# Layer-norm operands loaded in four parts behind weight chunks, and the state-space shuffles issued from ScalarE, in a two-layer hybrid trunk

## The chip, the core and the metric

The kernel runs on one core of a Trainium2 chip. The metric is the device time of one execution in microseconds (us); lower is better. Five engines matter: TensorE (PE) multiplies, VectorE (DVE), ScalarE (ACT) and GpSimd (POOL) do elementwise work, and SyncE (SP) mostly issues DMA transfers. Each engine runs its instructions in the order in which they stand in its own queue, so an issue that must wait holds up all issues behind it.

## The reference

256 tokens of width 1024 pass through two layers. A layer mixes tokens in three ways (RWKV-7, latent attention, a diagonal state space model called S5), merges the three under gates, projects by `w_out`, adds the residual and normalizes; then a SwiGLU feed-forward network, residual and normalization again. All is in float32.

```python
for l in range(DEPTH):
    p = x @ w_in[l]
    ...
    merged = gates[..., 0, :] * y_a + gates[..., 1, :] * y_b + gates[..., 2, :] * y_c
    x = layer_norm(DEEPNORM_ALPHA * x + merged @ w_out[l], ln1_g[l], ln1_b[l])
    h = jax.nn.silu(x @ ffn_w1[l]) * (x @ ffn_w3[l])
    x = layer_norm(DEEPNORM_ALPHA * x + h @ ffn_w2[l], ln2_g[l], ln2_b[l])
```

## The kernel before

**Weights.** All large weights lie in one DRAM array of chunks, 138 per layer, most of them 128x1024 float32 (512 KB). `w_load` brings a chunk in: SP issues a DMA into `raw` (L160), ACT casts it to the high part `whi` (L161), DVE (for some columns POOL, L173) subtracts to get the low part `wlo` (L171). There are 3 buffers of `raw` and 4 of each part, and `w_next` keeps 4 chunks loaded ahead of use. Each product is three matmuls: high by high, high by low, low by high (L203 to L205; in `token_major` L487 to L489). So PE can run only as long as chunks arrive and are split, and a chunk's DMA can start only when the cast and the subtraction have freed one of the 3 `raw` buffers.

**The two projections that end in a normalization** are done by `token_major`: `w_out` with 8 chunks and the second FFN matrix ("ffn2") with 22. Tokens lie on partitions, and four accumulators of 128x512 are kept: two token blocks b0 and b1 by two column halves n0 and n1 (`mm`, `mm`, `mm`, and one named `pc`). The last four chunks are held, and the code runs them for b0n0, then b0n1, b1n0 and b1n1, so that `layer_norm` of b0 can begin while PE still works on b1. `layer_norm` adds the residual `xk` (L446), takes statistics (L448, L449), gets the inverse root (L235 on DVE, L237 on POOL), centres and scales by `lg` (L453), and scales and shifts by `lb` (L460). Then PE transposes the result (L467), ACT copies it out as `xh`, and DVE makes its low part `xl` (L470). The next product's first matmuls (L1270 to L1272 in ffn1) need both. The new residual is written to DRAM as `xd`, from which the next `token_major` loads it.

**The order** of instructions on each engine is set by a scheduler that may move an instruction ahead of others on its engine wherever data and buffers allow. That holds for the loads of `lg`, `lb` (512 KB each, one row repeated on all partitions) and `xk` (1 MB), which stand in `token_major` at step `k == at`: `at` is 2 for `w_out` and 12 for ffn2. Their memory comes from a pool that takes over space used by others before: for ffn2 of layer 0 that of temporaries (`st`, `ct`, `t`, L430 to L434) which POOL uses to make the sine tables of layer 1's S5.

**The S5 input.** The product `u` is copied out of PSUM by ACT (L113) and shuffled over partitions into `U2` by 8 DMAs of 64 KB each (L671, issued from SP), from which PE's first S5 products (L702) read.

Of the kernel before, what the change touches and what calls it, by code (L numbers as in the profile page):

```python
# [17 lines left out]
D = 1024  # L18
# [68 lines left out]
def trunk(ctx: ExitStack, tc: tile.TileContext, xT, xtok, ws, spA, spB, spC, sp5, lnv, cst, out, dbg=None,  # L87
          layers=L, mark=None):
    nc = tc.nc
    V, S, PE, SY, G = nc.vector, nc.scalar, nc.tensor, nc.sync, nc.gpsimd  # L90
# [14 lines left out]
    def mmps():  # L105
        return pmm.tile([128, 512], F32, tag="mm", name="mm")

    def mxps(k):
        return pmx.tile([128, 512], F32, tag="p" + k, name="p" + k, bufs=1 if k == "c" else 2)

    def cp(k, out, in_):

        {"S": S.copy, "V": V.tensor_copy, "G": G.tensor_copy}[CPE[k]](out=out, in_=in_)  # L113
# [36 lines left out]
    state = {"next": 0}  # L150
# [5 lines left out]
    def w_load(i, hi, lo):  # L156
        w = LAT if i in lat_chunks else CH
        raw = wp.tile([128, CH], F32, tag="raw", name="raw", bufs=WRAW)
        for s in (slice(0, w // 2), slice(w // 2, w)) if i == 0 else (slice(0, w),):
            SY.dma_start(out=raw[:, s], in_=ws[i, :, s])  # L160
            S.copy(out=hi[:, s], in_=raw[:, s])  # L161
            if i == 0:
                V.tensor_tensor(out=lo[:, s], in0=raw[:, s], in1=hi[:, s].bitcast(F32), op=ALU.subtract)
        if i == 0:
            return
        if gate:

            V.tensor_copy(out=lo[:, 0:1], in_=gate.pop())
        n, j = divmod(i, CHUNKS_PER_LAYER)
        m = w * int(GS[24 * n + j // 3]) // 8 if j < 72 else w  # L170
        V.tensor_tensor(out=lo[:, 0:m], in0=raw[:, 0:m], in1=hi[:, 0:m].bitcast(F32), op=ALU.subtract)  # L171
        if m < w:
            G.tensor_tensor(out=lo[:, m:w], in0=raw[:, m:w], in1=hi[:, m:w].bitcast(F32), op=ALU.subtract)  # L173

    def w_early(pool, i):

        w = LAT if i in lat_chunks else CH
        early[i] = t = pool.tile([128, w], F32R, name=f"eh{i}"), pool.tile([128, w], F32R, name=f"el{i}")
        w_load(i, *t)

    def w_prefetch():
        i = state["next"]
        if i >= nchunks:
            return
        state["next"] = i + 1
        if i not in early:
            hi = wp.tile([128, CH], F32R, tag="whi", name="whi", bufs=WHI)
            lo = wp.tile([128, CH], F32R, tag="wlo", name="wlo", bufs=WHI)
            w_load(i, hi, lo)
            wq.append((hi, lo))  # L190
        else:
            wq.append(early[i])

    def w_next(ahead=AHEAD):
        while sum(w not in early.values() for w in wq) < ahead:
            if state["next"] >= nchunks:
                break
            w_prefetch()
        return wq.pop(0)
# [20 lines left out]
    def proj_pair(x, nk=8):  # L220
        ps = mmps()
        for j in range(2):
            proj(w_next(), 0, x, nk, ps[:, 256 * j:256 * j + 256])
        return ps
# [19 lines left out]
    with tc.tile_pool(name="xin", bufs=1) as q:  # L244
        xr = q.tile([128, 8, T], F32, name="xr")
        for i in range(4):
            s = slice(2 * i, 2 * i + 2)
# [8 lines left out]
        for i in range(4):  # L256
            s = slice(2 * i, 2 * i + 2)
            S.copy(out=xh[:, s], in_=xr[:, s])
            V.tensor_tensor(out=xl[:, s], in0=xr[:, s], in1=xh[:, s].bitcast(F32), op=ALU.subtract)  # L259
    x_dram = xtok  # L260
# [213 lines left out]
    def token_major(a, nk, ln, last, q, l, at):  # L474

        nonlocal x_dram
        lg = q.tile([128, D], F32, tag="lg", name="lg")
        lb = q.tile([128, D], F32, tag="lb", name="lb")
        xk = q.tile([128, 2, D], F32, tag="xk", name="xk")
        acc = [[mmps(), mmps()], [mmps(), mxps("c")]]  # L480

        def run(w, k, b, ns=(0, 1)):
            t = slice(128 * b, 128 * b + 128)
            for n in ns:
                s = slice(512 * n, 512 * n + 512)
                ah, al = a[0][:, k, t], a[1][:, k, t]
                PE.matmul(acc[b][n], lhsT=ah, rhs=w[0][:, s], start=(k == 0), stop=False)  # L487
                PE.matmul(acc[b][n], lhsT=ah, rhs=w[1][:, s], start=False, stop=False)  # L488
                PE.matmul(acc[b][n], lhsT=al, rhs=w[0][:, s], start=False, stop=(k == nk - 1))  # L489

        for k in range(nk - NST):
            if k == at:
                SY.dma_start(out=lg, in_=lnv[l, ln:ln + 1, :].to_broadcast([128, D]))
                SY.dma_start(out=lb, in_=lnv[l, ln + 1:ln + 2, :].to_broadcast([128, D]))
                SY.dma_start(out=xk, in_=x_dram)
            w = w_next()
            for b in range(2):
                run(w, k, b)
        wst = [w_next(NST - i) for i in range(NST)]
        ln_ = []  # L500
        for b in range(2):
            for n in range(2):
                for i in range(NST):
                    run(wst[i], nk - NST + i, b, (n,))
            ln_.append(layer_norm(q, xk, b, acc[b], lg, lb, last, 4 * LN_EPS))
            next(ln_[b])
            if (LNL if last else LNO) == 0:
                next(ln_[b])
        if (LNL if last else LNO) == 1:
            next(ln_[0])  # L510
            next(ln_[1])
        if not last:
            xd = dr.tile([128, 2, D], F32, tag=f"xd{l}{ln}", name=f"xd{l}{ln}")
            SY.dma_start(out=xd, in_=xk)
            x_dram = xd
# [4 lines left out]
    for l in range(layers):  # L520
# [136 lines left out]
        with tc.tile_pool(name=f"s5p{l}", bufs=1, side=P) as q:  # L657
            u = q.tile([128, 4, 2, 128], F32, tag="u", name="u")
            U2 = q.tile([128, 8, 128], F32, tag="U2", name="U2")

            def s5_in(fp):
                mark("s5proj")
                ps = proj_pair(X)
                for i in range(2):
                    cp(5, out=u[:, 2 * fp:2 * fp + 2, i, :], in_=ps.rearrange("p (f c i) -> p f i c", f=2, i=2)[:, :, i, :])
                if fp == 0:
                    return
                for j in range(4):
                    for i in range(2):
                        r = 64 * (j % 2) + 32 * i  # L670
                        SY.dma_start(out=U2[r:r + 32, j // 2::2, :], in_=u[32 * j:32 * j + 32, :, i, :])  # L671

            tgen = []

# [78 lines left out]
            def s5_gelu(i):  # L753
# [7 lines left out]
                else:  # L761
# [5 lines left out]
                V.tensor_tensor(out=yS[1][:, s], in0=g, in1=yS[0][:, s].bitcast(F32), op=ALU.subtract)  # L767

            run = {"S": s5_in, "T": s5_tables0, "m": lat, "N": lambda _: mla_norm(q, lts[0]), "r": rw_unit, "P": layer_params, "t": s5_tile,
                   "g": s5_gelu, "G": lambda fp: gate_pair(2, fp, M[:, 2 * fp:2 * fp + 2])}  # L770
            gens = {}
# [30 lines left out]
        q = mixed.enter_context(tc.tile_pool(name=f"rw{l}", bufs=1, side=P))  # L802
        if True:
# [288 lines left out]
            for i in range(2):  # L1092
                r = slice(64 - 32 * i, 96 - 32 * i)
# [111 lines left out]
            gate0 = {}  # L1205
# [36 lines left out]
        dump("M", M)  # L1242
        with tc.tile_pool(name=f"mg{l}", bufs=1, side=P) as q:
            mark("wout")
            token_major(gate0[1], 8, 0, False, q, l, 2)
        gstack.close()


# [2 lines left out]
        with tc.tile_pool(name=f"ff{l}", bufs=1, side=O) as q:  # L1251
# [13 lines left out]
            for b in range(2):  # L1265
                ps = mmps()
                t = slice(128 * b, 128 * b + 128)
                for k in range(8):
                    w, s = w4[k // 2], slice(512 * (k % 2), 512 * (k % 2) + 512)
# [36 lines left out]
            with tc.tile_pool(name=f"mh{l}", bufs=1, side=P) as q2:  # L1306
                token_major((hh, hl), NF, 2, l == layers - 1, q2, l, 12)
# [181 lines left out]
```

## Time and profile before

| quantity | value |
|---|---|
| time, median of 3 runs | 1088.11 us (1084.67 to 1090.08) |
| profiled execution: time | 1090.58 us |
| profiled execution: span, first to last instruction | 1088.9 us |
| mean granted TensorE clock, share of full speed | 0.972 |
| PE busy | 1026.9 us (94%) |
| DVE / ACT / POOL busy | 802.8 / 477.3 / 231.5 us |
| chain of work that ended last | PE 61%, DVE 17%, POOL 10%, DMA 5%, ACT 3%, issue 3% |
| landing after issue, median: `raw` / `lg` / `lb` / `xk` from `xd` | 4.1 / 5.1 / 5.7 / 7.9 us |

The profiled execution took 2.47 us longer than the median run. Its span begins with the first instruction and ends with the last, 1.7 us short of the time. Times in the text such as "at 449" are us from the start of the span; layer 0 reaches to about 565, layer 1 from there on. Where a queue's row says xN, the N instructions stand behind one another and the length reaches to the end of the last.

### The profile page before, as it was taken

Reading aid. Unit: us, or ns where it says so; the run is one execution under the profiler, and the core shown is the slowest. Engines: PE = TensorE matmul, PEld = TensorE weight load, DVE = VectorE, ACT = ScalarE, POOL = GpSimd, SP = SyncE. Lnnn points to the kernel's source line nnn. Section 1 sums busy time; section 2 is a strip of 40 time slices with the busy share of each in tenths; the row PEclk is TensorE's granted clock in tenths of the full one; section 3 lists DMA queues with packets and bytes.
Section 4 is the critical chain, followed back from the end, with each engine's and each line's share of the span. In section 5 each row is a group of like instructions: output and inputs, shape, how many; then the busy total and the mean of one; then the engine's idle time right before and its main releaser. Section 6 shows DMA issues by size and latency. Waiting matters only on the chain.

```text
span 1088.9 us, 21216 instructions
## 1 busy us (share of the span) xinstructions
PE 1026.9 (94%) x8560; PEld 923.8 (85%) x8560; DVE 802.8 (74%) x1560; ACT 477.3 (44%) x789; POOL 231.5 (21%) x254
## 2 busy tenths in 40 slices
PE   9489999999999999899998999999999899999997
PEld 8378887888897899798878999878889779999985
DVE  7599988977478799576473898789756866676645
ACT  5243387544343344244325345765334433434331
POOL 2941042210000599400011003221002420000000
PEclk9789999999999999999998899999999999999999
DMA  7342262132285655466545325222225746555552
GB/s 279 98 140 86 95 192 73 59 118 96 81 291 183 204 173 167 178 209 217 184 143 177 115 80 173 90 97 79 79 98 169 243 152 230 186 183 180 186 195 78
DMA packets 47683, 164.91 MB, mean 151 GB/s; under 512 B 5729, under 2 KB 8289, under 8 KB 46689
## 3 DMA queue, kind: packets, MB, share of 16 engines
q1 hardware_dynamic: 47296, 163.03, 45.2%
q8 instruction: 67, 1.10, 0.4%
q10 hardware_dynamic: 288, 0.52, 0.1%
q14 instruction: 32, 0.25, 0.1%
HBM read 157.77 MB, written 4.19 MB: 149 GB/s over the span
## 4 chain that ended last, share of the span: by engine, by line
PE 61%; DVE 17%; POOL 10%; DMA 5%; ACT 3%; issue 3%; SPq 0%; DVEq 0%; ACTq 0%; POOLq 0%
PE mm L205 11%; PE mm L204 11%; PE mm L203 11%; DMA raw<-in_ws 4%; PE mm L488 3%; PE mm L489 3%; PE mm L487 3%; DVE wlo L171 3%; ACT whi L161 2%; DVE z L721 2%; POOL st L432 1%; POOL st L434 1%; PE pa L702 1%; POOL t L430 1%; PE pa L916 1%
## 5 line engine op out<-in xcount | busy, mean ns | idle before, releaser
L171 DVE TENSOR_TENSOR wlo<-raw,whi 128x1024 fp32r<-128x1024 f32 (+2 forms) x265 | 336.7, 1277 | 175.3 <-ACT whi L161 173.2
L161 ACT CAST whi<-raw 128x1024 fp32r<-128x1024 f32 (+2 forms) x267 | 277.5, 1043 | 386.0 <-PE mm L204 207.3
L203 PE MATMUL mm<-xh,whi 128*128 128x256 f32 x1312 | 379.5, 289 | 14.2 <-ACT whi L161 14.1
L205 PE MATMUL mm<-xh,wlo 128*128 128x256 f32 x1312 | 378.3, 289 | 2.1 <-DVE wlo L171 1.9
L204 PE MATMUL mm<-xl,whi 128*128 128x256 f32 x1312 | 379.3, 289 | 0.4 <-DVE xl L259 0.4
L203 PEld LDWEIGHTS mm<-xh,whi 128*128 128x128 f32 x1312 | 252.5, 192 | 18.7 <-ACT whi L161 14.7
L205 PEld LDWEIGHTS mm<-xh,wlo 128*128 128x128 f32 x1312 | 253.5, 193 | 6.1 <-DVE wlo L171 2.9
L204 PEld LDWEIGHTS mm<-xl,whi 128*128 128x128 f32 x1312 | 252.4, 192 | 3.9 <-issue 1.8
L237 POOL TENSOR_TENSOR rs<-rs,mhalf 128x1 f32<-128x1 f32 x8 | 7.8, 970 | 344.0 <-DVE rs L235 344.0
L203 PE MATMUL mm<-yh,whi 128*128 128x256 f32 x256 | 74.5, 291 | 0.1
L205 PE MATMUL mm<-yh,wlo 128*128 128x256 f32 x256 | 74.1, 290 | 0.0
L204 PE MATMUL mm<-yl,whi 128*128 128x256 f32 x256 | 74.1, 289 | 0.0
L488 PE MATMUL mm<-wlo,hh 128*128 128x512 f32 x132 | 52.0, 394 | 0.0
L487 PE MATMUL mm<-whi,hh 128*128 128x512 f32 x132 | 51.6, 394 | 0.0
L489 PE MATMUL mm<-whi,hl 128*128 128x512 f32 x132 | 51.5, 393 | 0.0
L203 PEld LDWEIGHTS mm<-yh,whi 128*128 128x128 f32 x256 | 48.5, 189 | 2.3 <-ACT qa L113 0.9
L204 PEld LDWEIGHTS mm<-yl,whi 128*128 128x128 f32 x256 | 48.5, 189 | 1.2 <-issue 0.8
L205 PEld LDWEIGHTS mm<-yh,wlo 128*128 128x128 f32 x256 | 48.6, 190 | 1.1 <-issue 0.7
L173 POOL TENSOR_TENSOR wlo<-raw,whi 128x384 fp32r<-128x384 f32 (+2 forms) x24 | 29.5, 1236 | 72.4 <-ACT whi L161 72.4
L237 POOL TENSOR_TENSOR rsn<-rsn,mhalf 128x8 f32<-128x8 f32 x4 | 6.5, 1634 | 142.8 <-DVE rsn L235 142.8
L923 POOL TENSOR_SCALAR_AFFINE_SELECT Mk<-Mk 64x512 f32<-64x512 f32 x32 | 27.0, 844 | 43.6 <-ACT Mk L113 42.3
L487 PEld LDWEIGHTS mm<-whi,hh 128*128 128x128 f32 x132 | 24.8, 188 | 6.1 <-DVE th L1260 0.7
(498 smaller groups left out, 1764.2 us busy)
## 6 DMA issues: line engine op xcount, KB each, us to landing
raw<-in_ws SPq DMA_DIRECT2D x267, 512.0 KB, 4.1
raw<-in_ws SPq DMA_DIRECT2D x8, 416.0 KB, 3.5
xd<-xk SPq DMA_DIRECT2D x3, 1024.0 KB, 4.1
xk<-xd SPq DMA_DIRECT2D x3, 1024.0 KB, 7.9
lg<-in_lnv SPq DMA_DIRECT2D x4, 512.0 KB, 5.1
lb<-in_lnv SPq DMA_DIRECT2D x4, 512.0 KB, 5.7
pc<-in_spC SPq DMA_DIRECT2D x2, 768.0 KB, 5.1
pb<-in_spB SPq DMA_DIRECT2D x2, 512.0 KB, 5.2
```

What stands on the lines that cost most here:

```text
L161: S.copy(out=hi[:, s], in_=raw[:, s])
L171: V.tensor_tensor(out=lo[:, 0:m], in0=raw[:, 0:m], in1=hi[:, 0:m].bitcast(F32), op=ALU.subtract)
L173: G.tensor_tensor(out=lo[:, m:w], in0=raw[:, m:w], in1=hi[:, m:w].bitcast(F32), op=ALU.subtract)
L203: PE.matmul(ps, lhsT=wh, rhs=xh, start=first, stop=False)
L204: PE.matmul(ps, lhsT=wh, rhs=xl, start=False, stop=False)
L205: PE.matmul(ps, lhsT=wl, rhs=xh, start=False, stop=last)
L237: G.tensor_tensor(out=out, in0=in_, in1=mh(out), op=ALU.pow)
L487: PE.matmul(acc[b][n], lhsT=ah, rhs=w[0][:, s], start=(k == 0), stop=False)
L488: PE.matmul(acc[b][n], lhsT=ah, rhs=w[1][:, s], start=False, stop=False)
L489: PE.matmul(acc[b][n], lhsT=al, rhs=w[0][:, s], start=False, stop=(k == nk - 1))
L721: V.tensor_tensor_scan(out=z[:, pp, qq, ri], data0=bc(m2[:, j:j + 1], [128, 128]), data1=z[:, pp, qq, ri], initial=0.0, op0=ALU.mult, op1= ...
L923: G.affine_select(out=Mk[r, h], in_=Mk[r, h], pattern=[[0, 4], [1, 2], [1, 64]], compare_op=ALU.is_ge, fill=0.0, base=-1, channel_multipli ...
```

## The change

The load of `lg`, `lb` and `xk` becomes four loads of 512 KB: the half of `xk` for b0, `lg`, `lb`, the half of `xk` for b1. One is issued at each of the steps k = at to at + 3, and `tc.issue_after` holds it in the queue behind the newest weight chunk's DMA (`state["dma"]`), so the scheduler cannot move it ahead. For `w_out`, `at` goes from 2 to 0; for ffn2 it stays 12. The 8 shuffles into `U2` are issued from ACT's queue instead of SP's.

```diff
@@ w_load
-            SY.dma_start(out=raw[:, s], in_=ws[i, :, s])
+            state["dma"] = SY.dma_start(out=raw[:, s], in_=ws[i, :, s])
@@ token_major
+        loads = [(xk[:, 0], x_dram[:, 0]), (lg, lnv[l, ln:ln + 1, :].to_broadcast([128, D])),
+                 (lb, lnv[l, ln + 1:ln + 2, :].to_broadcast([128, D])), (xk[:, 1], x_dram[:, 1])]
         for k in range(nk - NST):
-            if k == at:
-                SY.dma_start(out=lg, in_=lnv[l, ln:ln + 1, :].to_broadcast([128, D]))
-                SY.dma_start(out=lb, in_=lnv[l, ln + 1:ln + 2, :].to_broadcast([128, D]))
-                SY.dma_start(out=xk, in_=x_dram)
             w = w_next()
+            if at <= k < at + 4:
+
+                with tc.issue_after(state["dma"].ins if hasattr(state["dma"], "ins") else state["dma"]):
+                    SY.dma_start(out=loads[k - at][0], in_=loads[k - at][1])
@@ s5_in
-                        SY.dma_start(out=U2[r:r + 32, j // 2::2, :], in_=u[32 * j:32 * j + 32, :, i, :])
+                        S.dma_start(out=U2[r:r + 32, j // 2::2, :], in_=u[32 * j:32 * j + 32, :, i, :])
@@ the call for w_out
-            token_major(gate0[1], 8, 0, False, q, l, 2)
+            token_major(gate0[1], 8, 0, False, q, l, 0)
```

SP's queue in layer 0 between the table inputs of the next layer (`cd`) and the end of the layer held this before (a chunk of 832 columns is one of layer 1 that is loaded early, the others are those of ffn1 and ffn2):

```order
-L376 DMA cd<-in_spB 128x1024
-L160 DMA raw<-in_ws 128x1024 x22
-L493 DMA lg<-in_lnv 128x1024
-L494 DMA lb<-in_lnv 128x1024
-L495 DMA xk<-xd_4229 128x2048
-L160 DMA raw<-in_ws 128x1024 x14
-L160 DMA raw<-in_ws 128x832 x2
-L160 DMA raw<-in_ws 128x1024 x19
```

With the change the same stretch reads:

```order
+L376 DMA cd<-in_spB 128x1024
+L160 DMA raw<-in_ws 128x1024 x36
+L160 DMA raw<-in_ws 128x832 x2
+L160 DMA raw<-in_ws 128x1024 x13
+L498 DMA xk<-xd_4230 128x1024
+L160 DMA raw<-in_ws 128x1024
+L498 DMA lg<-in_lnv 128x1024
+L160 DMA raw<-in_ws 128x1024
+L498 DMA lb<-in_lnv 128x1024
+L160 DMA raw<-in_ws 128x1024
+L498 DMA xk<-xd_4230 128x1024
 L160 DMA raw<-in_ws 128x1024 x3
```

The 2 MB that stood in one block, 22 chunks behind `cd`, now stand 51 chunks behind it, in ffn2, each part between two chunks.

In layer 1 the end of `w_out` and ffn1 read so before (`xd_6293` is the residual of `w_out`, `xd_10152` that of ffn2; `lg` for `w_out` stands right ahead of this piece):

```order
 L160 DMA raw<-in_ws 128x1024 x3
-L494 DMA lb<-in_lnv 128x1024
-L160 DMA raw<-in_ws 128x1024 x3
-L495 DMA xk<-xd_6293 128x2048
-L160 DMA raw<-in_ws 128x1024 x9
-L493 DMA lg<-in_lnv 128x1024
-L160 DMA raw<-in_ws 128x1024 x2
-L494 DMA lb<-in_lnv 128x1024
-L160 DMA raw<-in_ws 128x1024
-L514 DMA xd_10152<-xk 128x2048
-L160 DMA raw<-in_ws 128x1024 x3
```

and now the loads of `w_out` stand so, with those of ffn2 another 53 chunks behind:

```order
+L160 DMA raw<-in_ws 128x1024 x35
+L498 DMA xk<-xd_6295 128x1024
+L160 DMA raw<-in_ws 128x1024
+L498 DMA lg<-in_lnv 128x1024
+L160 DMA raw<-in_ws 128x1024
+L498 DMA lb<-in_lnv 128x1024
+L160 DMA raw<-in_ws 128x1024
+L498 DMA xk<-xd_6295 128x1024
+L160 DMA raw<-in_ws 128x1024 x4
+L516 DMA xd_10155<-xk 128x2048
```

The 1 MB of `xk` for `w_out` stood 9 chunks ahead of the first load for ffn2, and that one (issued at 872.27) went out while PE still worked on `w_out`. Now only `w_out`'s own loads lie there, 5 to 12 chunks later than before.

The scheduler also changes PE's order at the end of `w_out` of layer 0 (`mm_4040` is the accumulator b0n0, `mm_4041` b0n1, `mm_4042` b1n0, `pc_4043` b1n1; `msh` and `msl` are the two parts of the merged input). Before, the two last matmuls for `mm_4040` and those that follow were these, with 24 more for b1 behind them:

```order
L488 MATMUL mm_4040<-wlo_4120,msh_3298 128x512
L489 MATMUL mm_4040<-whi_4119,msl_3299 128x512
L487 MATMUL mm_4041<-whi_4101,msh_3298 128x512
L488 MATMUL mm_4041<-wlo_4102,msh_3298 128x512
L489 MATMUL mm_4041<-whi_4101,msl_3299 128x512
L487 MATMUL mm_4041<-whi_4119,msh_3298 128x512
L488 MATMUL mm_4041<-wlo_4120,msh_3298 128x512
L489 MATMUL mm_4041<-whi_4119,msl_3299 128x512
```

Now the ten last matmuls of `w_out` are these:

```order
L488 MATMUL mm_4040<-wlo_4121,msh_3298 128x512
L489 MATMUL mm_4040<-whi_4120,msl_3299 128x512
L488 MATMUL mm_4041<-wlo_4121,msh_3298 128x512
L489 MATMUL mm_4041<-whi_4120,msl_3299 128x512
L488 MATMUL mm_4042<-wlo_4121,msh_3298 128x512
L489 MATMUL mm_4042<-whi_4120,msl_3299 128x512
L489 MATMUL pc_4043<-whi_4101,msl_3299 128x512
L487 MATMUL pc_4043<-whi_4120,msh_3298 128x512
L488 MATMUL pc_4043<-wlo_4121,msh_3298 128x512
L489 MATMUL pc_4043<-whi_4120,msl_3299 128x512
```

The last matmul for b0n0 stood 30 matmuls ahead of the end and now stands 8 ahead of it; that of b0n1 24, now 6; b1n0 12, now 4. In layer 1 the same distances go from 36, 24 and 12 to 18, 16 and 12.

## Rows read from the trace of the kernel before

**Rows 1.** Part 1 of the page: busy us of the engines (share of the span).

```profile
PE 1026.9 (94%) x8560; PEld 923.8 (85%) x8560; DVE 802.8 (74%) x1560; ACT 477.3 (44%) x789; POOL 231.5 (21%) x254
```

**Rows 2.** Timeline of SP's queue, 430 to 465: start, length, instructions.

```profile
430.28 6.84 SPq L160 DMA_DIRECT2D raw<-in_ws  x3
449.29 0.33 SPq L493 DMA_DIRECT2D lg<-in_lnv  x1
...
450.14 0.42 SPq L495 DMA_DIRECT2D xk<-xd  x1
450.67 13.72 SPq L160 DMA_DIRECT2D raw<-in_ws  x5
```

**Rows 3.** Chain that ended last, 445 to 470: start, length, what.

```profile
447.12 2.15 POOL st L434
...
450.67 8.25 DMA raw<-in_ws
...
460.10 1.24 DVE wlo L171
```

**Rows 4.** Windows: PE, PEld, DVE, ACT, POOL busy (x); clock, DMA share, GB/s.

```profile
455.50:460.20 4.70, 0.15 (x2) 0.08 (x1) 0.10 (x1) 1.18 (x2) 0.00 (x0) 1.00 0.98 404
460.20:467.20 7.00, 6.42 (x29) 6.12 (x30) 6.80 (x12) 3.51 (x5) 0.00 (x0) 0.51 0.51 173
467.20:478.00 10.80, 10.80 (x92) 10.80 (x91) 8.34 (x13) 4.76 (x6) 0.00 (x0) 1.00 0.78 227
```

**Rows 5.** Timeline of PE, 350 to 362: start, length, line, [idle before <-releaser].

```profile
352.78 0.40 PE L489 MATMUL pc<-whi,msl 128*128 128x512 f32 x1
353.02 1.04 PE L467 MATMUL pa<-c,xk 128*128 128x128 f32 x8
354.59 0.50 PE L1270 MATMUL mm<-eh,xh 128*128 128x512 f32 x1 [0.53 <-ACT xh L113]
...
355.31 0.50 PE L1272 MATMUL mm<-eh,xl 128*128 128x512 f32 x1
```

**Rows 6.** Timeline of DVE, 344 to 360, the same columns.

```profile
346.21 0.69 DVE L446 SCALAR_TENSOR_TENSOR xk<-xk,mm 128x512 f32<-128x512 f32 x1 [0.97 <-PE mm L489]
...
349.38 1.41 DVE L453 SCALAR_TENSOR_TENSOR xk<-xk,mv,lg 128x512 f32<-128x512 f32 x2
...
354.57 0.69 DVE L470 TENSOR_TENSOR xl<-pa,xh 128x512 fp32r<-128x512 f32 x1
```

**Rows 7.** Windows, columns of rows 4, over other stretches.

```profile
859.20:890.60 31.40, 26.16 (x99) 20.33 (x99) 21.20 (x29) 10.56 (x12) 11.64 (x8) 0.89 0.57 188
865.40:878.00 12.60, 12.52 (x47) 9.85 (x47) 7.52 (x8) 4.19 (x4) 6.25 (x4) 0.86 0.77 245
591.00:607.00 16.00, 16.00 (x66) 14.43 (x67) 6.40 (x12) 2.95 (x4) 0.00 (x0) 0.50 0.26 81
300.00:320.00 20.00, 20.00 (x169) 20.00 (x169) 13.76 (x17) 9.29 (x12) 2.13 (x5) 1.00 0.86 305
```

**Rows 8.** Timeline of PE, 858 to 896.

```profile
865.37 0.50 PE L487 MATMUL mm<-whi,msh 128*128 128x512 f32 x1 [3.18 <-DVE gate L796]
```

**Rows 9.** Chain that ended last, 846 to 896.

```profile
850.28 7.37 DMA raw<-in_ws
...
871.89 6.16 DMA raw<-in_ws
...
892.85 0.50 PE mm L1272
```

**Rows 10.** Timeline of SP's queue, 580 to 612.

```profile
587.07 5.12 SPq L671 DMA_DIRECT2D U<-u  x8
```

**Rows 11.** Timeline of PE, 585 to 594.

```profile
590.91 1.19 PE L702 MATMUL pa<-U,bl 64*128 64x128 f32 x4 [3.99 <-DMA U<-u]
```

**Rows 12.** Timeline of ACT, 583 to 600.

```profile
597.29 1.04 ACT L161 CAST whi<-raw 128x1024 fp32r<-128x1024 f32 x1 [7.66 <-PE mm L204]
```

**Rows 13.** Timeline of PE, 40 to 80.

```profile
55.86 0.31 PE L413 MATMUL pb<-cd,bd 128*32 128x32 f32 x2 [7.33 <-DVE bd L383]
```

## The prediction

> **What bounds the kernel now.** The page's first part comes first: PE is busy 94% of the span [rows 1], so only places where PE stands still, or runs at a lower clock, can give time back, and any new stand costs its full length. I then looked for PE's idle gaps near the instructions that the change touches: the loads in layer 0's ffn1, the two ends of `w_out`, and the shuffles of layer 1. (Layer numbers are 0 and 1.)
>
> The largest gap is at 449. SP issued its last chunk DMA before it at about 437, and then nothing until 449.29, when `lg` went out [rows 2]. The chain of waits says why: it runs through POOL's `st L434`, which ends at 447.12 + 2.15 = 449.27 [rows 3]. That is the last of the sine-table operations whose temporaries lie in the memory that `lg` is to take. So `lg` waited for POOL, and every chunk behind it in SP's queue waited too, though the chunks themselves had free buffers. Then 2 MB of `lg`, `lb` and `xk` travelled ahead of the next chunk, which was issued at 450.67 and took 8.25 us to land; its low part ended at 461.34 [rows 3]. The windows show what PE lost: nearly no work for 4.7 us, then 7.0 us with 29 matmuls at a granted clock of 0.51, near the lower level of 1.2 GHz, then 92 in 10.8 us at full clock (2.4 GHz), or 0.117 us each [rows 4].
>
> At the end of `w_out` of layer 0 PE hardly stands still: the last matmul is issued at 352.78, the transposes follow at 353.02, and the first matmul of ffn1 that needs `xl` (L1272) starts at 355.31 [rows 5]. DVE began to normalize b0 at 346.21, seven us ahead of PE's end [rows 6]; that is what the order "b0n0 first" buys.
>
> In layer 1 `w_out` takes 31.4 us [rows 7] for 96 matmuls. At the pitch between the rows at 352.78 and 353.02, 0.24 us, they need 23.0: 8.4 us are lost there. The chain names two chunk DMAs with long flights, 7.37 us and 6.16 us [rows 9]. The first left SP right behind the 1 MB of `xk`; the second travelled with ffn2's `lg`. The first delays ACT and DVE and so the gate product on which PE waits 3.18 us [rows 8], and at 865.4 to 878 the clock is 0.86 [rows 7].
>
> **The change, part by part.** I count gains as positive.
>
> *Layer 0, loads of ffn2.* They move 29 chunks later, past the end of the tables. Chunks at 437 to 450 no longer wait for POOL. In the 11.7 us of the first two windows of [rows 4] PE did 2 + 29 = 31 matmuls, worth 31 x 0.117 = 3.6 us at full clock: 8.1 us lost, and **+8.0** taken, with +6 (half of the slow-clock part comes back elsewhere) to +9 as bounds. The work that hides the loads at their new place is PE's: a ffn2 chunk is 12 matmuls of 0.24 us, 2.8 us, and at the 404 GB/s of the loaded window [rows 4] a chunk plus a 512 KB load takes 2 x 1.3 = 2.6 us. So the parts just fit, with four chunks in reserve; if they do not, see the second rival.
>
> *Layer 0, loads of `w_out`.* Before, they cost nothing: in 300 to 320 PE is busy 20.00 of 20 us [rows 7]. Now they stand among `w_out`'s own chunks, with the same 2.6 against 2.8 us. I take 0 for the transfer. But the scheduler's new order of PE has a price. The last matmul of b0n0 stands 8 ahead of the end in place of 30, so DVE starts about 8 x 0.24 - 0.1 = 1.8 us ahead of PE's end E, not 7.0. Before, from the start of the first L446 to the start of L470 it took 354.57 - 346.21 = 8.36 us [rows 6]. Now three more instructions of b1 stand in front of that L470 on DVE: two L453 (1.41 us together [rows 6]) and one more statistics or aggregate step of about 0.2 to 0.7 us. That makes about 9.9. The low part of b0 starts at E - 1.8 + 9.9 = E + 8.1 and ends 0.69 later, at E + 8.8; L1272 follows. Before it started at 355.31, which is E + 2.13 with E = 353.18 (352.78 + 0.40). So **-6.7**, with bounds -5 and -8. PE stands still for most of it. What the clock then does is bounded by three rows: after an idle of 3.18 us the next 12.6 us ran at 0.86, a loss of 12.6 x 0.14 = 1.8 us [rows 7, 8]; after the stand at 449 7.0 us ran at 0.51, a loss of 3.4 [rows 4]; after 3.99 us idle 16 us ran at 0.50, a loss of 8 [rows 7, 11]. I take **-2.0**, near the first, since PE has transposes and a few matmuls inside its idle time; bounds 0 and -8.
>
> *Layer 1, `w_out`.* Its own loads come 5 to 12 chunks later and those of ffn2 are out of it. The two flights exceed the median of 4.1 us by 3.3 and 2.1, together 5.4 us; all of the loss is 8.4. I take **+7.0**, since the lower clock comes with the waits, and keep +3 (its own four loads now travel with the last chunks) to +8.4. The tail costs here as well: b0n0 ends 18 matmuls ahead of the end, so DVE starts about 18 x 0.24 - 0.2 = 4.1 us ahead of E. With b1's statistics less crowded than in layer 0, L446 to the end of L470 is the 9.05 us of before (355.26 - 346.21), so `xl` is there at E + 4.95. Before, L1272 started at 892.85 [rows 9] with E = 890.60 (the end of the window in [rows 7]), so at E + 2.25: **-2.7** (0 to -4), and **-0.8** for the clock (0 to -1.8).
>
> *ffn2 of layer 1.* Later loads, same arithmetic as in layer 0's ffn2: 0.
>
> *Shuffles.* In layer 1 SP spends 5.12 us on the eight issues [rows 10]. The relief is worth nothing to SP, whose chunk DMAs are short of buffers, not of issue time. ACT can carry the issues: its next cast waits 7.66 us for PE anyway [rows 12], and without that cover the 5.12 us would be the cost. PE waits 3.99 us for `U2` [rows 11]. The first shuffle is issued when ACT's copy is done, from either queue; I take **0**, with 0 and +4 as bounds (all of the wait), +12 if the 16 us at clock 0.50 behind it [rows 7] come back as well.
>
> The Trainium skill, page "DMA: Bandwidth & Descriptors", section "Issuing engines are not separate DMA queues", says the same of any such move: transfers from SP and ACT run on the same 16 DMA engines, and a second issuer saves only the time to issue. By that rule the sum has 0 here too, or 5.12 us if SP's issue time were on the path, which the row of ACT's wait for PE speaks against.
>
> *Shuffles, layer 0.* There DVE's, ACT's and POOL's order around 45 to 65 is rearranged as well. PE stands 7.33 us for DVE's `bd` product [rows 13]; now DVE makes one `bd` ahead of a chunk's low part and that low part later. I take **0**, with 3 us either way.
>
> Sum: 8.0 - 6.7 - 2.0 + 7.0 - 2.7 - 0.8 = **+2.8 us**. The profiled execution would go from a span of 1088.9 to 1086.1, and from 1090.58 to 1087.8. It lies 2.47 above the median, so against the median I expect **1085.3 us**: a real gain at 449 and in layer 1's `w_out`, mostly given back behind the two first normalizations. A measurement of this kernel can tell about 0.5%, 5.4 us, from no change.
>
> **The rivals.**
>
> 1. *Shuffles faster.* For it: the chunk DMA stands right ahead of the shuffles in SP's ring. From ACT's they would not queue behind it. If PE then stands still too shortly for the clock to fall, the 16.0 us of [rows 7] become 66 x 0.117 = 7.7. Against it: idles of 3.18 us already drew the lower clock. Price +8.3: 1077.0. The skill's page "DMA: Bandwidth & Descriptors", section "Queues, rings and completion order", says that a DMA engine takes turns between queues packet by packet, which is the mechanism of this rival; no run so far shows it. Chance 0.13.
> 2. *The four places collide (slower).* Loads of 512 KB now lie between the last chunks in both `w_out` and both ffn2. With 3 `raw` buffers a chunk comes every (flight + cast 1.04 [rows 12] + low part 1.24 [rows 3]) / 3. That must stay under 2.8 us, so a flight over 6.2 us decides. At the 8.25 of [rows 3] it is 3.5, 0.7 late per chunk, 4 chunks in 4 places: -11 us, 1096. Against it: only 0.5 MB travels ahead of each chunk, not 2 MB: 4.1 + 1.3 = 5.4. Chance 0.12.
> 3. *The clock stays low behind layer 0's normalization* for 16 us, as behind the shuffles: 6 us more, 1091. Chance 0.10.
> 4. *The 449 gain does not come,* because some other chunk or load waits for the tables: 8 less, 1093.3. Speaks for it: the temporaries must still be free before `lg` lands somewhere. Against: it is needed 29 chunks later. Chance 0.08.
> 5. *The tail is not paid,* DVE being ahead of what the order suggests: +8.7, 1076.6. Chance 0.12.
>
> **How the numbers follow.** The forecast has 0.45. Rivals 1 and 5 end faster by over 0.5% (below 1082.7), and about 0.07 of the forecast's: 0.32. Slower (over 1093.5): all of rival 2, half of rival 4, a quarter of 3, and a little of the forecast: 0.20. Within: 0.48. The range reaches to rivals 1 and 5 below and to rivals 3 and 4 above, leaving rival 2 out: **1077 to 1094**.
>
> **What the profile of after would show.** Right: no SP gap at 437 to 449 and no clock of 0.5 at 460; `w_out` of layer 1 in about 24 us; in layer 0 a PE gap of some 6 us behind `w_out`, ended by ACT's `xh` or DVE's `xl`; L702 in layer 1 waiting about 4 us as before. Wrong: chunk flights over 6 us in ffn2 or `w_out` with PE waiting on `whi` (rival 2), or the clock at full behind 591 (rival 1).

## The result and the profile after

The changed kernel is slower: 1091.96 us median (1081.61 to 1096.49, 12 runs) against 1085.26 us for the kernel before on the same chips (1081.09 to 1090.08, 12 runs), a ratio of 1.0055 with a 95% interval of 1.0031 to 1.0079. That is 6 us more, 3 to 9 by the interval. With more runs the kernel before settled at 1085 to 1086, so the 1088.11 of the first three runs was high, and its profiled execution (1090.58) was one of the slowest of all. The profiled execution of the changed kernel took 1094.60 us with a span of 1092.9, 4.0 us more than that of before.

Part 1 of the page for the changed kernel, busy time of each engine:

```profile
PE 1025.6 (94%) x8560; PEld 925.0 (85%) x8560; DVE 801.0 (73%) x1560; ACT 478.0 (44%) x789; POOL 231.8 (21%) x254
```

PE works as long as before [rows 1]; the shares hardly differ. So the stretches must be compared. A timeline of SP's queue, 400 to 470:

```profile
401.51 66.79 SPq L160 DMA_DIRECT2D raw<-in_ws  x22
```

Twenty-two chunk DMAs and nothing between them: the hole of [rows 2] is gone, as is the stand at 449 to 467. In windows of the changed kernel (columns as in [rows 4]):

```profile
355.50:361.00 5.50, 0.30 (x2) 0.14 (x2) 5.50 (x13) 0.99 (x1) 0.95 (x1) 0.89 0.00 0
361.00:367.00 6.00, 6.00 (x21) 4.67 (x22) 5.20 (x11) 1.76 (x3) 1.00 (x1) 0.53 0.13 55
442.00:449.00 7.00, 4.32 (x67) 3.81 (x60) 6.86 (x8) 4.18 (x8) 7.00 (x5) 0.76 0.55 176
449.00:460.00 11.00, 11.00 (x94) 11.00 (x93) 7.96 (x10) 3.65 (x5) 8.19 (x6) 1.00 0.49 150
892.00:899.00 7.00, 6.33 (x20) 4.94 (x19) 6.49 (x14) 1.17 (x2) 1.00 (x1) 0.52 0.13 54
```

From 449 to 460 PE is busy all the time at full clock, where before it stood or crawled from 455.5 to 467.2 [rows 4]. But the other four rows are new losses: PE idle at 355.5 to 361 and at the lower clock at 361 to 367 (0.53), idle for 2.7 us within 442 to 449 (4.32 of 7 us busy, clock 0.76), and at the lower clock again at 892 to 899 (0.52). The first answers to [rows 5]. PE, and below it DVE, at the end of `w_out` of layer 0:

```profile
355.27 0.40 PE L489 MATMUL pc<-whi,msl 128*128 128x512 f32 x1
360.86 1.97 PE L467 MATMUL pa<-c,xk 128*128 128x128 f32 x8 [5.20 <-DVE xk L460]
...
363.67 0.71 PE L1274 MATMUL mm<-eh,xl 128*128 128x512 f32 x1
```

```profile
353.84 1.29 DVE L446 SCALAR_TENSOR_TENSOR xk<-xk,mm 128x512 f32<-128x512 f32 x2 [2.83 <-PE mm L489]
...
357.56 1.41 DVE L453 SCALAR_TENSOR_TENSOR xk<-xk,mv,lg 128x512 f32<-128x512 f32 x2
358.88 1.28 DVE L448 BATCH_NORM_STATS2 st<-xk 128x6 f32<-128x512 f32 x2
...
362.85 0.68 DVE L470 TENSOR_TENSOR xl<-pa,xh 128x512 fp32r<-128x512 f32 x1
```

The last matmul of `w_out` starts at 355.27, and PE then waits 5.20 us for DVE's L460. DVE started b0 at 353.84, 1.8 us ahead of PE's end at 355.67, and not seven ahead as in [rows 6]. It works through the extra pieces (both L448 of b1, another pair of L453) and reaches the first L470 at 362.85. L1274, the matmul that stood at L1272 before, starts at 363.67, 8.0 us behind PE's end; before, that was 2.1 us [rows 5].

The idle time at 442 was not in the prediction at all. PE waits for ACT's copy `bl`, a table product of layer 1's S5:

```profile
445.11 1.97 PE L404 MATMUL pa<-c,bd 128*128 128x128 f32 x8 [2.68 <-ACT bl L113]
```

The chain of waits leads back from there:

```profile
437.58 4.29 DVE wlo L171 x2
...
444.20 0.38 ACT th L1260
444.58 0.48 ACT bl L113
```

ACT's `bl` copy stands in its queue behind `th` (L1260), which waits for a DVE chain that begins with two low parts (4.29 us). In the kernel before, the copy stood behind `th` as well, but at another point of ffn1's work (432.89), where PE waited only 0.78 us. After the wait the lower clock stands for 3.4 us.

In layer 1 `w_out` lasts 27.0 us from the start of its first matmul to the end of its last, not 31.0 (the window of 31.4 in [rows 7] opens 0.4 us ahead of that matmul), but the wait for the gate product stays nearly as long as in [rows 8]:

```profile
867.18 0.50 PE L487 MATMUL mm<-whi,msh 128*128 128x512 f32 x1 [3.09 <-DVE gate L798]
```

The chain of waits shows that no long flight is behind it now (4.34 us against the 7.37 of [rows 9]), and that DVE ends it; and that at the end of `w_out` the chain runs through DVE's L460 into PE's transposes at 891.76:

```profile
857.39 4.34 DMA raw<-in_ws
...
866.20 0.34 DVE msh L113
866.53 0.61 DVE gate L798
...
891.76 0.68 PE pa L467 x4
...
893.10 0.79 PE mm L1272
```

The shuffles in layer 1: ACT, and PE's wait for `U2`:

```profile
591.16 5.25 ACTq L673 DMA_DIRECT2D U<-u  x8
596.46 0.84 ACT L647 ACTIVATE mlain<-pb,pa 128x256 f32<-128x256 f32 x2 [5.06 <-issue]
```

```profile
594.04 0.68 PE L704 MATMUL pa<-U,bl 64*128 64x128 f32 x4 [2.46 <-DMA U<-u]
```

ACT stands 5.06 us in its issues; PE's wait is 2.46 us, less than the 3.99 of [rows 11].

In layer 0 the new order makes PE stand 16.9 us in one piece for DVE's `bd`, where it stood 7.3 [rows 13]. What this is worth is seen below in `u2_l0`. PE's waits up to 100 us:

```profile
PE pb L413 <- DVE bd L383: 16.9, 1, 16.9
```

### The profile page after: what moved, and what is told of

Its sections match the earlier page's. It is cut to its first block, busy times and chain, and to the rows that moved or that the text cites. A ratio compares the mean times of both kernels' runs of the same rounds, so it can differ in the third digit from the quotient of the medians.

```text
span 1092.9 us, 21231 instructions
## 1 busy us (share of the span) xinstructions
PE 1025.6 (94%) x8560; PEld 925.0 (85%) x8560; DVE 801.0 (73%) x1560; ACT 478.0 (44%) x789; POOL 231.8 (21%) x254
## 4 chain that ended last, share of the span: by engine, by line
PE 67%; DVE 20%; DMA 4%; ACT 3%; POOL 3%; issue 3%; ACTq 0%; DVEq 0%; SPq 0%; POOLq 0%
PE mm L203 12%; PE mm L205 12%; PE mm L204 12%; DVE wlo L171 4%; PE mm L487 4%; PE mm L488 4%; DMA raw<-in_ws 4%; PE mm L489 3%; DVE z L723 2%; ACT whi L161 1%; PE pa L918 1%; PE pb L1013 1%; PE pc L488 1%; PE pc L489 1%; PE pc L487 1%
## 5 line engine op out<-in xcount | busy, mean ns | idle before, releaser
L171 DVE TENSOR_TENSOR wlo<-raw,whi 128x1024 fp32r<-128x1024 f32 (+2 forms) x265 | 336.5, 1276 | 166.3 <-ACT whi L161 163.4
L205 PEld LDWEIGHTS mm<-xh,wlo 128*128 128x128 f32 x1312 | 250.9, 191 | 7.5 <-DVE wlo L171 4.9
L173 POOL TENSOR_TENSOR wlo<-raw,whi 128x384 fp32r<-128x384 f32 (+2 forms) x24 | 31.4, 1309 | 70.9 <-ACT whi L161 70.3
L488 PEld LDWEIGHTS mm<-wlo,hh 128*128 128x128 f32 x132 | 24.8, 188 | 5.9 <-DVE wlo L171 0.6
```

Of the source, the lines that this page charges most:

```text
L205: PE.matmul(ps, lhsT=wl, rhs=xh, start=False, stop=last)
```

## The experiments

All ratios are to the kernel before, with 95% intervals. Because the clock differs from execution to execution (below), a verdict rests on the timed ratios, and profiles only show where something happens. Each ratio rests on 12 runs of its kernel, but on 9 of `ffn2_only`, 8 of `f_tail` and 6 of `f_free4`, against 12 to 35 runs of the kernel before. Two stretches were measured in every profile, from PE's first `w_out` matmul to its first ffn2 matmul, in layer 0 and in layer 1:

| kernel | ratio | interval | layer 0, us | layer 1, us |
|---|---|---|---|---|
| before | 1 | | 168.1 | 160.7 |
| the change | 1.0055 | 1.0031 to 1.0079 | 168.9 | 161.9 |
| u2_only | 1.0042 | 1.0019 to 1.0065 | 168.1 | 157.5 |
| loads_only | 1.0012 | 0.9988 to 1.0037 | 169.8 | 158.4 |
| ffn2_only | 0.9930 | 0.9902 to 0.9957 | 160.4 | 157.3 |
| wout_only | 1.0031 | 0.9995 to 1.0066 | 169.8 | 157.8 |
| u2_l0 | 1.0002 | 0.9981 to 1.0023 | 167.1 | 157.6 |
| u2_l1 | 1.0039 | 1.0015 to 1.0062 | 167.9 | 160.4 |
| f_tail | 1.0058 | 1.0025 to 1.0090 | 167.0 | 163.4 |
| f_free4 | 0.9892 | 0.9866 to 0.9918 | 159.7 | 156.6 |
| u2_l1_pool | 1.0059 | 1.0030 to 1.0088 | 168.5 | 157.8 |
| after_free4 | 0.9953 | 0.9926 to 0.9980 | 160.0 | 157.7 |
| f_w1pin | 0.9956 | 0.9925 to 0.9987 | 160.2 | 158.2 |
| f_free4_pool | 0.9945 | 0.9924 to 0.9966 | 159.3 | 156.3 |

**The change in its parts.** Four kernels, each with part of the change. `u2_only`: the shuffles on ACT, all loads as before. `loads_only`: all loads as in the change, the shuffles back on SP. `ffn2_only` and `wout_only`: one of the two load edits alone.

```diff
 u2_only:    loads as before;  S.dma_start(out=U2[...])
 loads_only: -S.dma_start(out=U2[...])  +SY.dma_start(out=U2[...])
 ffn2_only:  +if ln == 2 and at <= k < at + 4: (pinned, four parts)   w_out as before, at = 2
 wout_only:  +if ln == 0 and at <= k < at + 4: (pinned, four parts)   ffn2 as before, at = 12
```

> The kernel before, with only the eight shuffles moved to ACT's queue. Theory A (the loss of the change comes from pinning w_out's loads, which turns the order at the end of both w_out): ratio 0.998 to 1.003, no part of the loss. Theory B (the shuffles on ACT, and the new order at the start of layer 0 that comes with them, cost the loss): 1.004 to 1.008, with the gap before the first matmul of the second input chunk at 37 to 54 us as in the changed kernel and the wait for U2 in layer 1 near 2.5 us. Theory C (ffn2's loads collide with ffn2's chunks): 1.000.

> The changed kernel with the shuffles back on SP. Theory A: the whole loss stays, ratio 1.003 to 1.008. Theory B: 0.995 to 1.000. Theory C: as A, 1.003 to 1.008, but with PE waiting for chunks inside ffn2.

> The kernel before, with only ffn2's loads in four pinned parts; w_out's loads and the shuffles as before. Theory A: the gain at 449 comes without the price, 8 us in layer 0 and 1 to 4 us in layer 1's w_out, ratio 0.988 to 0.993; the order at the end of w_out is that of before. Theory B: the same, 0.988 to 0.993. Theory C: 0.998 to 1.008, with idle gaps of PE in ffn2 behind the four loads.

> The kernel before, with only w_out's loads in four pinned parts (from the first step); ffn2's loads and the shuffles as before. Theory A: the price without the gain: idle of 5 us behind w_out in layer 0 and 2 to 3 us in layer 1 plus the low clock behind each, less 1 to 4 us inside w_out, while the stall at 449 stays: ratio 1.006 to 1.013. Theory B: 0.997 to 1.002. Theory C: 0.997 to 1.002.

Measured: shuffles alone 1.0042, all loads alone 1.0012; together they make the 1.0055 of the change. Theory A (the whole loss lies in `w_out`'s loads) fell in this form, and so did theory B (the whole loss lies in the shuffles). The shuffles cost 4 to 5 us, and for the loads, which should have gained, no gain is measured (the interval reaches from 1.3 us of gain to 4.0 of loss). Theory C fell: ffn2's loads alone gain 0.7%. In that kernel they go out between chunks like this (SP's queue):

```profile
516.50 0.38 SPq L502 DMA_DIRECT2D xk<-xd  x1
518.88 0.33 SPq L160 DMA_DIRECT2D raw<-in_ws  x1
519.25 0.42 SPq L502 DMA_DIRECT2D lg<-in_lnv  x1
```

and PE stays busy in ffn2. The windows of the same kernel show both a stretch around the old stand of 449 and the stretch behind the shuffles of layer 1:

```profile
446.00:462.00 16.00, 16.00 (x136) 16.00 (x134) 13.29 (x16) 6.18 (x9) 4.05 (x3) 1.00 0.57 192
582.00:598.00 16.00, 16.00 (x126) 15.12 (x125) 11.08 (x23) 5.90 (x8) 0.00 (x0) 1.00 0.55 174
```

`wout_only` holds a surprise: its stretch in layer 0 is as long as that of the whole change, so it pays the tail (the wait behind `w_out` for the late `b0n0`), yet the stand at 449 is gone there too, though ffn2's loads are where they were. SP's queue:

```profile
395.88 51.78 SPq L160 DMA_DIRECT2D raw<-in_ws  x17
455.56 0.33 SPq L495 DMA_DIRECT2D lg<-in_lnv  x1
```

The tables end later, `lg` waits for them until 455.56, but the chunk before it had been issued at 447.66, so the hole is 8 us and not 12, and the chunks in reserve cover it. What PE waits for at 330 to 480 in that kernel, over 1 us, is only this (total us, times, longest):

```profile
PE pa L467 <- DVE xk L460: 5.2, 1, 5.2
PE pa L404 <- ACT bl L113: 2.7, 1, 2.7
```

Both load edits remove the same stand, which is why they should not add up; by the ratios they would give 0.9961, and 1.0012 was measured.

**The late end of b0n0 by itself.** `f_tail` takes `ffn2_only` and changes only the order of multiplication in both `w_out`: chunk by chunk, so b0n0, b0n1 and b1n0 end 9, 6 and 3 matmuls ahead of the end. No load moves. `f_w1pin` pins `w_out`'s loads in layer 1 alone.

```diff
 f_tail:
+        if ln == 0:
+            for i in range(NST):
+                for b in range(2):
+                    run(wst[i], nk - NST + i, b)
-                for i in range(NST):
+                for i in range(0 if ln == 0 else NST):
 f_w1pin:
+            if (ln == 2 or l == 1) and at <= k < at + 4: (pinned; at = 0 in layer 1, 2 in layer 0)
```

> The kernel with only ffn2's loads pinned (ratio 0.993 to before), and in both w_out the last four chunks multiplied chunk by chunk instead of accumulator by accumulator, so that b0n0 ends 9 matmuls ahead of the end; no load of w_out is moved. Theory A (the price of pinning w_out's loads is the late end of b0n0): PE idle of 4 to 5 us behind w_out in layer 0 and 4 us or more in layer 1, low clock behind both, ratio 0.999 to 1.004 to before. Theory F (the price is in the loads' transfer itself and the later tables): 0.992 to 0.995, as without this edit.

> Only ffn2's loads pinned (0.993), and w_out's too in layer 1, but not in layer 0. Theory A by layer: in layer 1 the later end of b0n0 (18 matmuls ahead of the end) costs 2.5 to 3 us of idle and the low clock behind it, against 2 to 4 us saved inside w_out: 0.991 to 0.996. So nearly the whole price of the pinning lies in layer 0, with the wait at 442 that follows from it.

Measured for `f_tail`: 1.0058, that is 1.3% or 14 us slower than `ffn2_only`, more than the 6 to 12 us expected. Its profile repeats the pattern of the change, the wait for L460 in both layers and the wait for `bl` as well (waits of PE, 330 to 896):

```profile
PE pa L467 <- DVE xk L460: 10.2, 2, 5.1
...
PE pa L404 <- ACT bl L113: 2.8, 1, 2.8
```

So the order of multiplication alone, with no load moved, makes the idle time behind `w_out` in both layers; the wait for `bl` comes with it, as in every profile with the late end in layer 0. Of the 14 us the profiles show 6.6 in layer 0's stretch and 6.1 in layer 1's. `f_w1pin` gives 0.9956, 0.3% above `ffn2_only`, but the two intervals overlap: a price of layer 1's pinning is not shown, and it is far below that of `f_tail`. Its gap behind `w_out` of layer 1 and the window after it:

```profile
875.25 0.66 PE L467 MATMUL pa<-c,xk 128*128 128x128 f32 x4 [2.45 <-DVE xk L460]
```

```profile
875.00:882.00 7.00, 6.07 (x34) 4.96 (x35) 7.00 (x16) 2.06 (x4) 1.00 (x1) 1.00 0.09 37
```

The idle time is the 2.45 us of the change, but this time the clock stayed at 1.00 behind it.

**The shuffles by layer and by queue.** `u2_l0` and `u2_l1` move them in one layer only; `u2_l1_pool` issues those of layer 1 from GpSimd, which is idle then.

```diff
 u2_l0:      (S if l == 0 else SY).dma_start(out=U2[...])
 u2_l1:      (S if l == 1 else SY).dma_start(out=U2[...])
 u2_l1_pool: (G if l == 1 else SY).dma_start(out=U2[...])
```

> The kernel before, with the shuffles moved to ACT's queue in layer 0 only. Moving them in both layers cost 0.42%. Theory D (the cost lies in layer 0, where ACT, DVE and PE run in another order and PE stands 16.9 us in one piece): ratio 1.002 to 1.006. Theory E (it lies in layer 1, where the input projection and the copy of u stand in another order): 0.999 to 1.001.

> The kernel before, with the shuffles moved to ACT's queue in layer 1 only. Theory D: 0.998 to 1.001. Theory E: 1.002 to 1.006.

> The kernel before, with the shuffles of layer 1 issued from GpSimd, which is idle there, and not from ACT (which cost 0.39%). Theory G (the cost is ACT standing 5 us in its own issues, so that the casts and copies behind them come late): 0.998 to 1.001. Theory H (the cost is taking the shuffles out of SP's queue, so that they travel beside the chunks and not behind them): 1.002 to 1.005, as from ACT.

Measured: 1.0002 in layer 0, 1.0039 in layer 1, 1.0059 from GpSimd. The price lies in layer 1, and theory G fell: without ACT's 5 us of issuing it is no smaller. A new order of instructions is not the price either: from GpSimd ACT's order in the trace is that of before, and PE's first product from `U2` stands one matmul later. With GpSimd ACT goes on with `mlain` at once, but PE waits longer for `U2`:

```profile
590.90 0.64 ACT L113 COPY u<-mm 128x256 f32<-128x256 f32 x2
591.42 0.85 ACT L653 ACTIVATE mlain<-pb,pa 128x256 f32<-128x256 f32 x2
```

```profile
596.55 1.19 PE L710 MATMUL pa<-U,bl 64*128 64x128 f32 x4 [5.20 <-DMA U<-u]
```

Theory H (what costs is that the shuffles leave SP's queue and travel beside the chunks) is what is left, though 1.0059 lies above its 1.002 to 1.005. The traces show that they do so. On SP no chunk goes out until the eight shuffles are issued [rows 10]. From GpSimd SP issues two chunks among them; landing after issue of the eight is the third line here, and the fourth is the same for the kernel before:

```profile
591.57 4.56 POOL L679 DMA_DIRECT2D U<-u  x8 [5.46 <-ACT u L113]
592.28 3.49 SPq L160 DMA_DIRECT2D raw<-in_ws  x2
DMA to landing us min/median/max: 2.9/3.5/4.1
DMA to landing us min/median/max: 2.0/2.1/3.5
```

In layer 1 the median flight of a shuffle was 2.0 to 2.2 us in the eight profiles with those shuffles on SP, 2.6 to 3.3 in the four with them on ACT (one chunk among them each time), and 3.5 and 3.9 in the two with them on GpSimd. But in `u2_l0` the shuffles of layer 0 fly longer too (3.3 for 2.1), at no price in time. PE's wait for `U2` in layer 1 was 2.0 to 4.0, 2.5 to 4.9, and 5.1 and 5.2 us, in the same order.

**Putting together what gains.** `f_free4` takes `ffn2_only` and sends `w_out`'s loads in four parts too, but not pinned. `after_free4` is the whole change with only that difference, and `f_free4_pool` is `f_free4` with layer 1's shuffles from GpSimd.

```diff
 f_free4:
+            if ln == 0 and at <= k < at + 4:
+                SY.dma_start(out=loads[k - at][0], in_=loads[k - at][1])
             w = w_next()
 after_free4: the same with S.dma_start(out=U2[...])
 f_free4_pool: the same with (G if l == 1 else SY).dma_start(out=U2[...])
```

> The kernel with only ffn2's loads pinned, and w_out's loads in four parts that the scheduler may move ahead. The order at the end of w_out stays that of before. If the 1 MB of xk in one piece is what delays the chunk ahead of the gate product in layer 1 (3 us of PE idle there), that wait shrinks to under 1.5 us and the ratio to before is 0.988 to 0.991; if the wait comes from ACT's and DVE's own work it stays, 0.992 to 0.994.

> The changed kernel with only the pinning of w_out's loads taken away: they stay in four parts, free to be moved ahead by the scheduler; ffn2's loads pinned, shuffles on ACT. If the parts add up, the gain of the free parts (ratio 0.989) and the price of the shuffles on ACT (1.004) give 0.991 to 0.995. A ratio of 0.999 or more would say that the shuffles and not the pinning hold back the gain.

> The best version so far (ffn2's loads pinned, w_out's in four free parts, 0.989), with the shuffles of layer 1 issued from GpSimd. Theory G: 0.986 to 0.991, no loss. Theory H: 0.991 to 0.995.

Measured: 0.9892, 0.9953 and 0.9945. `f_free4` has the lowest time of the study (1077.24 us median, 6 runs), but its interval overlaps that of `ffn2_only`, so a gain from the free parts is not shown. The scheduler moves its first loads of layer 0 far ahead and keeps b0n0 at 30 and 36 matmuls ahead of the end. The wait for the gate product shrank to 2.18 us and not to under 1.5, so the 1 MB of `xk` in one piece is not shown to be what makes it (in `after_free4`, with the same loads, it was 4.25 us):

```profile
848.64 0.50 PE L487 MATMUL mm<-whi,msh 128*128 128x512 f32 x1 [2.18 <-DVE gate L804]
```

The other two are 0.5 to 0.6% above it, of the size seen in `u2_l1` and `u2_l1_pool`: the price of the shuffles outside SP's queue, a third time and a fourth. Their intervals and that of `f_free4` (up to 0.9918, from 0.9924) just fail to touch, and they were timed in another set of runs.

## Why the prediction was wrong

It forecast 2.8 us of gain, as a sum of terms that nearly cancel; the parts measured on the chip are a loss of 1.3 us for the loads (0.12%, with an interval that holds zero but not 2.8 us of gain) and one of 4.6 for the shuffles (0.42%). Two of its terms failed: the 0 for the shuffles and the +7.0 for layer 1's `w_out`.

**Layer 0's loads: right in sum, in part by luck.** +8.0, -6.7 and -2.0 gave -0.7 for the stretch from `w_out` to ffn2; the profiles give 168.1 and 168.9, -0.8. The +8.0 is confirmed by `ffn2_only` (168.1 to 160.4, 7.7) and by the four other kernels with ffn2's loads pinned and the old order at the end of layer 0's `w_out` (159.3 to 160.2). The price of the tail, 8.7, is 6.6 by `f_tail` against `ffn2_only`, 8.5 and 9.4 by the change and by `loads_only`. Its composition was different: L1274 came 8.0 us behind PE's end and not 8.8, `w_out` itself ran 1.5 us shorter (25.9 to 24.4; before, some 34 of its matmuls came 0.27 us apart and not 0.23, for a reason not found), and the wait at 442 with the clock behind it took about 3.5, which no step named. That the sum came out is luck as far as these last two go.

**Layer 1: the +7.0 was mis-sized.** `w_out` gave back 4.0 us (31.0 to 27.0), since the wait for the gate product stayed (3.18 before, 3.09 after): moving the 1 MB away from ahead of it shortened the flight, not that wait. In the three other profiles with these loads pinned it was 1.71 to 2.71, so a part of it may come back; how much is open. So `w_out` came to 27.0 us, not to the 24 or so that was to be the sign of it. And the tail with the clock took 5.2, not 3.5. The larger fault was the source: the profiled execution of before was a bad one there. Four kernels leave `w_out` and its loads of layer 1 untouched; `u2_only`, `u2_l0` and `u2_l1_pool` need 157.5 to 157.8 us for the stretch where that profile showed 160.7 (27.8 to 28.1 for `w_out`, not 31.0), and only `u2_l1` needs 160.4. So in most of these profiles some 3 us of the 8.4 that the prediction called lost were not lost. The pinning that was to win them back shows no gain there by `f_w1pin`: 0.9956 against 0.9930, within the noise, and 158.2 us against 157.3 for the stretch.

**Shuffles: the 0 failed.** The step that failed is "The first shuffle is issued when ACT's copy is done, from either queue; I take 0", for layer 1; in layer 0 the 0 held (`u2_l0`, 1.0002). The wait for `U2` did not grow in the changed kernel, as forecast, and ACT's cover held, but the kernel is slower when the shuffles of layer 1 leave SP's queue, by 0.4% on ACT and 0.6% on GpSimd. Rival 1, the opposite of it, did not come. The rule of the Trainium skill that was weighed there (page "DMA: Bandwidth & Descriptors", section "Issuing engines are not separate DMA queues": another issuer saves only issue time) agrees with the missing gain, and says nothing of a loss, which the runs show.

The step overlooked what SP's queue does for the shuffles: there the next chunks stand behind them. Outside it a chunk goes out among them, and those behind it land later (median 2.1 us before, 3.0 in `u2_l1`, 3.5 in `u2_l1_pool`). How that becomes 4 to 6 us stays open. From GpSimd PE's wait for `U2` is longer by 1 to 3 us, from ACT not clearly. The low clock behind `U2` (13.7 to 17.1 us of it) is missing in 3 of 8 profiles with the shuffles on SP, and in none of the 6 others; with so few profiles that is a hint, not a proof. The mean granted clock of the timed runs does not settle it: 21% of the runs of before had 0.979 or more, none of `u2_only` and `u2_l1_pool`, but none of `loads_only` and `f_tail` either, whose shuffles leave from SP.

**The baseline.** The sum was made against an execution 5.3 us above the median that 12 runs gave. The forecast time of 1085.3 was therefore 0.0% from the kernel before as measured, not 0.3% faster. Rivals 2, 4 and 5 did not happen: no chunk held PE up in `w_out` or ffn2 for more than 0.6 us (though flights in layer 1's `w_out` reached 6.3 us, just over the 6.2 of rival 2), the gain at 449 came, the tail was paid. Rival 3 came in part: the clock fell behind both normalizations, for about 7 us each, not 16.

## What to carry to other kernels

When loads are pinned into a stage, look at what the scheduler does to the rest of it: here the end of one accumulator moved 22 matmuls, and in `f_tail` such an order alone, in both layers, costs 1.3%, more than the 0.7% that pinning ffn2's loads gained. Loads that nobody needs soon (ffn2's) can be pinned late; those needed at the end of layer 0's `w_out` were better left free, whole or in parts. Small transfers on which PE waits lost here by leaving the queue in which large loads stood behind them. And terms of a sum read from a single profile should be checked against how much that stretch differs between executions, before several of them are added to a difference of 3 us.

## What the runs showed of the hardware

The granted clock differs between executions of the same kernel, by chance as far as these runs show. Runs of the kernel before ranged from 1076.42 to 1091.16 us in one set of 35, and over the 13 changed kernels a run was on average 0.85 us longer for each 0.001 of mean clock that it had less than its kernel's mean. The stretch behind the shuffles of layer 1 shows it best. In `f_free4` PE waited 2.80 us for `U2`, and then:

```profile
583.00:599.00 16.00, 16.00 (x124) 15.11 (x125) 10.81 (x22) 5.21 (x8) 0.00 (x0) 1.00 0.53 163
```

That is 124 matmuls in 16 us at 1.00, the level of 2.4 GHz; the kernel before did 66 at 0.50 [rows 7] after 3.99 us of waiting. But the changed kernel, with a wait of only 2.46 us, got the lower clock for 13.7 us. So the length of the wait alone did not decide, and 8 us hang on it.
